# Seven-product form in the output projection and in two of three FFN-output stages

## The chip, the cores and the metric

One core of one Trainium2 chip runs the kernel, as one launch. The metric is the device time of one execution in microseconds (us). Repeated runs of the kernel before agree within 0.11% (1417.35 to 1418.89 us).

## What is computed

One encoder layer over 256 tokens and 2048 channels, all float32:

```
h   = rms_norm(x);  proj = h @ w_in            # q/k/v of three attention mixers and three gates
merged = sum over branches of sigmoid(gate_i) * (attention_i @ w_br_i)
x   = x + merged @ w_o                         # output projection, 2048 x 2048
hf  = rms_norm(x) @ w_ffn_in                   # 2048 -> 2 * 5632
x   = x + (silu(hf[:, :5632]) * hf[:, 5632:]) @ w_ffn_out   # 5632 -> 2048
```

## The kernel before

**Precision.** TensorE multiplies in a reduced float32 format. So each operand is held as a rounded part `hi` and a remainder `lo`, and one product of a 128x128 stationary tile by a 128x512 moving tile is three matmuls: hi·hi, hi·lo, lo·hi (`mul` in `pair`). The activations are stationary, transposed (channels on partitions); the weights move. Weight tiles arrive as 512 KB loads (`raw`, two k-tiles of 512 columns). `halves` splits each into `whi` (a copy on ScalarE, ACT, L351) and `wlo` (a subtraction on VectorE, DVE, L352).

**A pair.** `pair` makes the product of all 256 tokens (two token tiles t) with two column blocks c of 512, over k in pairs u of k-tiles. One u in one c is a *whole* step: 2 k-tiles x 2 token tiles x 3 = 12 matmuls; steps `du` and `Du` are c = 0 and 1. The four results lie in the PSUM banks Y, V (c = 0) and Z, Q (c = 1).

**The seven-product form.** For one u, the two k-tiles, two token tiles and two column blocks are a 2x2 by 2x2 block product: eight products, 24 matmuls, by the steps d and D. The form of Strassen and Winograd makes do with seven, 21 matmuls, at the price of sums. The step `f` makes two products (banks X, Y) from the c = 0 weights. `g` makes three DVE sums of weights (L441 to L443), then two products (W, Z). `h` makes one more sum (L457) and one product (V). `p` and `q` make the last two products (both X) from the sums kept in `t2` and `t3`, for up to two u at once. The stationary operands of W, Z and X are sums of token blocks, the *forms*; `stationary_forms` makes them in advance (L706 to L712, then a split). At the end of such a pair X is copied three times and W once (ACT, L392), DVE subtracts twice (L475, L478), and `sums` adds these to Y, V, Z, Q (L399, L400), so that `done` finds its result in SBUF. Without seven-product steps `done` reads PSUM itself.

**Order.** A pair's steps are a list (`STEPS`, `STEPS_GATE`, `STEPS_FFN`; `whole_k` has only d and D). `run` emits what a step needs (load, sums, split) three steps (`AHEAD`) before its matmuls; there are four buffers each of `whi` and `wlo`, and six of `raw`. Matmuls and SyncE's loads keep program order; `nc.follow` keeps the weight sums and splits of one engine in order; a planner places everything else. `tick` advances one side job after each step: work that follows a pair, such as the transposes, is such a job, under high priority.

**Stages around the change.** `merging`: gate pairs (3 of 8 u in seven-product form) and branch pairs. `projecting`: two pairs by `w_o`, all whole steps; its `add` adds the result to x (L764), then x is squared (ACT, L770), transposed and split into x1T (L124, L125). `feeding`: three groups of hidden columns (4, 4 and 3 pairs by `w_ffn`, all with 3 of 8 u in seven-product form); after each group two pairs by `w_ffn_out`, all whole steps, whose `output` adds the result to x (L818). The hidden activations are transposed by `transposed` and split into hT (L121, L122).

Of the kernel before, what the change touches and what calls it, by code (L numbers as in the profile page):

```python
# [49 lines left out]

SEVEN = (1, 2, 3)
STEPS = "d0 f1 D0 g1 d4 h1 f2 D4 g2 d5 h2 f3 D5 g3 d6 h3 p0 p2 D6 q0 q2 d7 D7".split()
STEPS_GATE = "d0 D0 d4 D4 f1 d5 g1 D5 h1 f2 g2 d6 h2 f3 g3 h3 p0 p2 D6 q0 q2 d7 D7".split()
STEPS_FFN = "d0 D0 f1 d4 g1 D4 h1 f2 d5 g2 D5 h2 f3 d6 g3 h3 p0 p2 D6 q0 q2 d7 D7".split()
AHEAD = 3


# [38 lines left out]
def encoder_block(ctx: ExitStack, tc: tile.TileContext, a: dict, out: bass.AP):  # L98
# [12 lines left out]
    def s4(shape, name, dt=F32):  # L111
        return mid.tile(shape, dt, name=name, tag="s4")
# [148 lines left out]
        row_scale(sr, r)  # L261
        known.add(name)

    def transposed(src, dst, g=None, lag=1):

        for h in range(2):
            if h:
                yield lag
            tp = bank("tp", "mm" if h and nc.on else "at")
            for k in range(2):  # L270
                for t in range(T):
                    nc.tensor.transpose(tp[:, k * S + t * P:k * S + (t + 1) * P],
                                        src[t][:, (2 * h + k) * P:(2 * h + k + 1) * P], ident)
# [82 lines left out]
    def pair(src, lhs, order, done, forms=None, operand=None):  # L356
# [5 lines left out]

        seven = sum(o[0] == "f" for o in order)
        left = {"X": 3 * seven}
        for o in order:
            for b in {"f": "Y", "g": "WZ", "h": "V", "d": "YV" * 2, "D": "ZQ" * 2}.get(o[0], ""):
# [69 lines left out]
        def second(u):  # L438
            def ready():
                b1, b2 = held[u]  # L440
                nc.follow(nc.vector.tensor_add(t3[:, SEVEN.index(u)], b2[:, 0], b2[:, 1]))  # L441
                nc.follow(nc.vector.tensor_add(b2[:, 0], b2[:, 0], b1[:, 0]))  # L442
                nc.follow(nc.vector.tensor_add(t2[:, SEVEN.index(u)], b2[:, 0], b2[:, 1]))  # L443
                hi, lo = halves(b2)

                def products():
                    mul("W", forms(u, 0), hi[:, 0], lo[:, 0])
                    mul("Z", forms(u, 2), hi[:, 1], lo[:, 1])
                    if left["W"] == 0:
                        copy(("B", 1), "W")  # L450
                return products
            return ready

        def third(u):
            def ready():
                b1 = held.pop(u)[0]
                nc.follow(nc.vector.tensor_add(b1[:, 1], t2[:, SEVEN.index(u)], b1[:, 1]))  # L457
                hi, lo = halves(b1[:, 1])
                return lambda: mul("V", at(2 * u + 1, 1), hi[:, 0], lo[:, 0])
            return ready  # L460

        def rest(o, v):
            tt, f = (t2, 1) if o == "p" else (t3, 3)
            n = min(2, seven - v)

            def ready():
                hi, lo = halves(tt[:, v:v + n])

                def products():
                    for i in range(n):  # L470
                        mul("X", forms(SEVEN[v + i], f), hi[:, i], lo[:, i])
                    if v + n == seven:
                        if o == "p":
# [217 lines left out]
    mT, x1T, x = [], [], []  # L691
    ss1 = const.tile([P, T, 4], F32, name="ss1")

    def stationary_forms(lhs, pool=None):


        n = len(SEVEN)
        fh = s8([P, 4, n, P], "fh", pool=pool)
        fl = s8([P, 4, n, P], "fl", pool=pool)
        raw = s8([P, 4, n, P], "fraw", F32)  # L700
        full = s8([P, 2 * n, S], "ffull", F32)

        def steps():
            for i, u in enumerate(SEVEN):
                for k in range(2):
                    nc.vector.tensor_add(full[:, 2 * i + k], *(v.bitcast(F32) for v in lhs(2 * u + k)))  # L706
            yield 1
            b = full.rearrange("p (u k) (t s) -> p k t u s", k=2, t=2)
            nc.vector.tensor_sub(raw[:, 0], b[:, 0, 1], b[:, 1, 1])
            nc.vector.tensor_sub(raw[:, 3], b[:, 0, 0], b[:, 0, 1])  # L710
            nc.vector.tensor_sub(raw[:, 1], raw[:, 0], b[:, 0, 0])
            nc.vector.tensor_add(raw[:, 2], raw[:, 1], b[:, 1, 0])  # L712
            yield 1
            split(fh, fl, raw)
        start(steps())
        return lambda u, f: (fh[:, f, SEVEN.index(u)], fl[:, f, SEVEN.index(u)])

    def merging():
        forms = stationary_forms(xT, tail)
        for b, (g0, k0, k1) in enumerate(((8, 2, 6), (4, 6, 12))):  # L720
            for j in (0, 2):
                sg = [None, None]
# [29 lines left out]
    forms = []  # L752


    def projecting():
        x.extend(s8([P, D], f"x{t}", F32) for t in range(T))
        for t in range(T):
            nc.sync.dma_start(out=x[t], in_=a["x"][t * P:(t + 1) * P, :])
        x1T.extend(s8([P, 2, 4, S], "x1T") for _ in range(4))
        for n in (0, 2):  # L760
            def add(c, r, n=n):
                xc = [x[t][:, (n + c) * NC:(n + c + 1) * NC] for t in range(T)]
                for t in range(T):
                    nc.vector.tensor_add(xc[t], r[t], xc[t])  # L764

                def later():
                    yield 1
                    sq = s4([P, T, NC], "sq")
                    for t in range(T):
                        nc.scalar.activation(sq[:, t], xc[t], AF.Square, accum_out=ss1[:, t, n + c:n + c + 1])  # L770
                    yield 2
                    yield from transposed(xc, lambda k, m: (x1T[n + c][:, 0, k], x1T[n + c][:, 1, k]),
                                          lambda k: gT[:, 2, 4 * (n + c) + k:4 * (n + c) + k + 1], 2)
                    if n + c == 1:
                        forms.append(stationary_forms(x1l))
                    elif n + c == 3:
                        yield 2
                        ssr = small.tile([P, T], F32, name="ss", bufs=1)
                        nc.vector.tensor_reduce(ssr, ss1, axis=AX.X, op=ALU.add)
                        row_scale(ssr, r_f)  # L780
                start(urgent(later()))
            yield pair(block_pair(a["w_o"], n), lambda k: (mT[k // 4][:, 0, k % 4], mT[k // 4][:, 1, k % 4]),
                       whole_k(KT // 2), add)


    def feeding():
        for c0, c1 in ((0, 4), (4, 8), (8, KF // 4)):
            hT = []
            for n in range(c0, c1):
                halves_of = []  # L790

                def hidden(c, v, av=halves_of):
                    if c == 0:
                        av.append(v)
                        for t in range(T):
# [6 lines left out]
                    def later():  # L802
# [1 line left out]
                        nc.vector.tensor_mul(av, av, bv)  # L804
                        yield 3
                        yield from transposed([av[:, t] for t in range(T)],
                                              lambda k, m: (tl[:, 0, k:k + m], tl[:, 1, k:k + m]), lag=2)
                    start(urgent(later()))
                yield pair(lambda u, c, n=n: a["w_ffn"][n][2 * u + c], x1l, STEPS if n else STEPS_FFN, hidden,
                           lambda u, f: forms[0](u, f))  # L810
            last = c1 == KF // 4
            for n in (0, 2):
                def output(c, r, n=n, last=last):
                    for t in range(T):
                        for h in range(2 if last and n + c == 3 else 1):
                            w = NC if not (last and n + c == 3) else NC // 2
                            o = slice((n + c) * NC + h * w, (n + c) * NC + (h + 1) * w)
                            nc.vector.scalar_tensor_tensor(x[t][:, o], r[t][:, h * w:(h + 1) * w],  # L818
                                                           r_f[:, 0, t:t + 1], x[t][:, o],
                                                           op0=ALU.mult, op1=ALU.add)  # L820
                            if last:
                                nc.sync.dma_start(out=out[t * P:(t + 1) * P, o], in_=x[t][:, o])
                yield pair(lambda u, c, n=n, c0=c0: a["w_ffn_out"][n + c][2 * c0 + u],
                           lambda k, hT=hT: (hT[k // 4][:, 0, k % 4], hT[k // 4][:, 1, k % 4]),
                           whole_k(2 * (c1 - c0)), output)

    def everything():
        for stage in (merging, projecting, feeding):
# [88 lines left out]
```

## Time and profile before

| | |
|---|---|
| runs | 1417.35, 1418.86, 1418.89 us; median 1418.86 |
| the profiled execution | 1419.69 us, of which the span of the profile is 1417.9 us |
| PE busy | 1395.6 us, 98% of the span |
| DVE busy | 1033.6 us, 73% |
| ACT busy | 764.9 us, 54% |
| memory traffic | 277 MB, 195 GB/s |

Matmuls overlap in the profile: one of 128x512 is shown as some 0.39 us, but the next begins 0.23 us after it. A matmul's cost is therefore read as the distance between starts. A busy share is an average over the stretch that it stands for.

### The profile page before, as it was taken

What the parts mean: (1) busy time and instruction counts of PE and PEld (TensorE: products, weight loads), DVE (VectorE), ACT (ScalarE), POOL (GpSimd) and SP (SyncE); (2) the same over time, 40 slices, a digit from 0 to 9 for tenths busy, and PEclk for the clock granted to TensorE, in tenths of its full rate; (3) what the DMA queues carried; (4) which work ended last, traced back from release to release, by engine and by line L of the source; (5) the groups of instructions that cost most, each with busy time, mean ns of one, the idle gap of its engine ahead of it and who ended that gap; (6) DMA issues with size and microseconds to landing.
All of it is one profiled execution on the core that took longest, in us unless ns stands there. A gap on an engine that the chain in (4) does not pass through costs nothing.

```text
span 1417.9 us, 17330 instructions
## 1 busy us (share of the span) xinstructions
PE 1395.6 (98%) x6287; PEld 1144.8 (81%) x6287; DVE 1033.6 (73%) x1305; ACT 764.9 (54%) x1026; POOL 76.7 (5%) x146
## 2 busy tenths in 40 slices
PE   8999999999999999999999999999999999999998
PEld 6778878888878888888878888888888888888886
DVE  5767756765588887767788897548889845788854
ACT  6766546644464564645565556335566633465632
POOL 0024533200000000000000000000000000000000
PEclk9999999999999999999999999999999999999999
DMA  8976535546565675765555666665566666555644
GB/s 287 334 240 212 161 109 190 157 154 195 178 196 178 193 225 173 273 187 180 175 183 192 203 193 213 192 193 181 191 193 204 215 190 193 180 191 191 221 127 174
DMA packets 79414, 277.07 MB, mean 195 GB/s; under 512 B 8992, under 2 KB 11552, under 8 KB 79072
## 3 DMA queue, kind: packets, MB, share of 16 engines
q1 hardware_dynamic: 79184, 275.94, 60.1%
q8 instruction: 49, 0.80, 0.2%
q14 instruction: 37, 0.30, 0.1%
q10 hardware_dynamic: 144, 0.02, 0.0%
HBM read 273.05 MB, written 2.88 MB: 195 GB/s over the span
## 4 chain that ended last, share of the span: by engine, by line
PE 84%; DVE 5%; ACT 3%; issue 3%; DMA 2%; POOL 2%; SPq 0%; ACTq 0%; DVEq 0%; POOLq 0%
PE mm L73 17%; PE mmZ L73 15%; PE mmV L73 14%; PE mmY L73 14%; PE mmQ L73 13%; PE mmX L73 6%; DVE wlo L352 3%; ACT whi L351 2%; PE mmW L73 2%; DMA raw<-in_w_mem 1%; PE tp L73 1%; PE sc L73 1%; POOL rot L571 1%; DVE raw L442 1%; DVE t L441 1%
## 5 line engine op out<-in xcount | busy, mean ns | idle before, releaser
L352 DVE TENSOR_TENSOR wlo<-raw,whi 128x1024 fp32r<-128x1024 f32 (+1 forms) x441 | 509.6, 1168 | 249.1 <-ACT whi L351 245.0
L351 ACT ACTIVATE whi<-raw 128x1024 fp32r<-128x1024 f32 (+1 forms) x441 | 437.4, 1013 | 403.0 <-PE mmV L73 133.7
L73 PE MATMUL mm<-whi,xT 128*128 128x512 f32 x768 | 243.9, 394 | 0.0
L122 DVE TENSOR_TENSOR wlo<-raw,whi 128x1024 fp32r<-128x1024 f32 x100 | 128.5, 1295 | 80.8 <-ACT whi L121 80.6
L73 PEld LDWEIGHTS mm<-whi,xT 128*128 128x128 f32 x768 | 144.0, 189 | 29.5 <-issue 0.8
L121 ACT ACTIVATE whi<-raw 128x1024 fp32r<-128x1024 f32 x100 | 105.7, 1070 | 88.1 <-PE mm L73 81.4
L73 PE MATMUL mm<-wlo,xT 128*128 128x512 f32 x384 | 150.7, 393 | 0.0
L73 PE MATMUL mmY<-whi,x1T 128*128 128x512 f32 x286 | 111.2, 390 | 0.0
L73 PE MATMUL mmV<-whi,x1T 128*128 128x512 f32 x286 | 108.6, 392 | 0.0
L73 PE MATMUL mmZ<-whi,x1T 128*128 128x512 f32 x220 | 85.7, 389 | 0.0
L73 PE MATMUL mmQ<-whi,x1T 128*128 128x512 f32 x220 | 85.6, 389 | 0.0
L73 PEld LDWEIGHTS mm<-wlo,xT 128*128 128x128 f32 x384 | 72.5, 189 | 15.7 <-issue 0.8
L73 PE MATMUL mmZ<-whi,hT 128*128 128x512 f32 x176 | 69.6, 395 | 0.0
L73 PE MATMUL mmQ<-whi,hT 128*128 128x512 f32 x176 | 69.1, 393 | 0.0
L73 PE MATMUL mmV<-whi,hT 128*128 128x512 f32 x176 | 69.1, 392 | 0.0
L73 PE MATMUL mmY<-whi,hT 128*128 128x512 f32 x176 | 69.1, 392 | 0.0
L73 PEld LDWEIGHTS mmY<-whi,x1T 128*128 128x128 f32 x286 | 53.7, 188 | 11.3
L73 PEld LDWEIGHTS mmV<-whi,x1T 128*128 128x128 f32 x286 | 53.7, 188 | 11.1 <-ACT whi L351 0.2
L352 DVE TENSOR_TENSOR wlo<-t,whi 128x1024 fp32r<-128x1024 f32 (+1 forms) x60 | 54.7, 953 | 3.9 <-ACT whi L351 3.9
L73 PE MATMUL mmV<-wlo,x1T 128*128 128x512 f32 x143 | 55.8, 390 | 0.2 <-DVE wlo L352 0.2
L73 PE MATMUL mmY<-wlo,x1T 128*128 128x512 f32 x143 | 55.7, 389 | 0.0
L351 ACT ACTIVATE whi<-t 128x1024 fp32r<-128x1024 f32 (+1 forms) x60 | 48.5, 834 | 0.0
(254 smaller groups left out, 2620.1 us busy)
## 6 DMA issues: line engine op xcount, KB each, us to landing
raw<-in_w_ffn SPq DMA_DIRECT2D x176, 512.0 KB, 3.7
raw<-in_w_gate SPq DMA_DIRECT2D x96, 512.0 KB, 4.1
raw<-in_w_ffn_out SPq DMA_DIRECT2D x88, 512.0 KB, 3.8
raw<-in_w_qkv SPq DMA_DIRECT2D x64, 512.0 KB, 4.6
raw<-in_w_o SPq DMA_DIRECT2D x32, 512.0 KB, 3.6
raw<-in_w_br SPq DMA_DIRECT2D x24, 512.0 KB, 3.7
raw<-in_w_mem SPq DMA_DIRECT2D x16, 512.0 KB, 6.6
rawT<-in_memT SPq DMA_DIRECT2D x8, 256.0 KB, 4.8
```

Source lines behind the costliest of these rows:

```text
L73: ins = op(*args, **kw)
L121: nc.scalar.activation(hi, src, AF.Copy)
L122: nc.vector.tensor_sub(lo, src, hi.bitcast(F32))
L351: nc.follow(nc.scalar.activation(hi[:, o], v, AF.Copy))
L352: nc.follow(nc.vector.tensor_sub(lo[:, o], v, hi[:, o].bitcast(F32)))
L441: nc.follow(nc.vector.tensor_add(t3[:, SEVEN.index(u)], b2[:, 0], b2[:, 1]))
L442: nc.follow(nc.vector.tensor_add(b2[:, 0], b2[:, 0], b1[:, 0]))
L571: op(ov[:, :, :, c], ov[:, :, :, c], tmp[:, :n])
```

## The change

Two seven-product steps (u = 2 and 3) take the place of four whole steps in both pairs of the output projection; two (u = 6, 7) and three (u = 5, 6, 7) in the two output pairs of the first and second FFN group. The third group's output pairs stay. The forms are now made one u at a time by `token_sums`, in four small operations and a split, in tiles of their own. For u = 6 and 7 of the hidden activations they are made from the transposes in PSUM (`also`); for the others from hi + lo.

```diff
-SEVEN = (1, 2, 3)
+STEPS_O = "d0 D0 d1 D1 f2 d4 g2 D4 h2 d5 f3 D5 g3 d6 h3 p0 D6 q0 d7 D7".split()
+STEPS_OUT = "d0 D0 d1 D1 d2 D2 f6 d3 g6 D3 h6 f7 d4 g7 h7 p0 D4 q0 d5 D5".split()
+STEPS_OUT2 = "d0 f5 D0 g5 d1 h5 f6 D1 g6 d2 h6 f7 D2 g7 d3 h7 p0 p2 D3 q0 q2 d4 D4".split()
...
-    def transposed(src, dst, g=None, lag=1):
+    def transposed(src, dst, g=None, lag=1, also=None):
...
                 split(d[0], d[1], tp.rearrange("p (k s) -> p k s", s=S))
+                if also:
+                    full = s4([P, 4, P], "ffull")
+                    nc.scalar.activation(full, tp.rearrange("p (b s) -> p b s", s=P), AF.Copy)
+                    also(h, full)
...
-    def stationary_forms(lhs, pool=None):
...
+    def token_sums(full, to):
+        raw = s4([P, 4, P], "fraw")
+        nc.vector.tensor_sub(raw[:, :2], full[:, :2], full[:, 1::2])
+        nc.vector.tensor_sub(raw[:, 2], raw[:, 1], full[:, 0])
+        nc.vector.tensor_add(raw[:, 3], raw[:, 2], full[:, 2])
+        split(to[:, 0], to[:, 1], raw)
+
+    def sums_of(lhs, these, room):
         def steps():
+            for u, to in zip(these, room):
+                full = s4([P, 4, P], "ffull")
                 for k in range(2):
+                    nc.vector.tensor_add(full[:, 2 * k:2 * k + 2].rearrange("p t s -> p (t s)"),
+                                         *(v.bitcast(F32) for v in lhs(2 * u + k)))
+                token_sums(full, to)
+                yield 1
         start(steps())
+        return by_pair(these, room)
...
     def merging():
-        forms = stationary_forms(xT, tail)
+        forms = sums_of(xT, (1, 2, 3), form_room(3, tail))
...
     def projecting():
+        oforms = sums_of(mTl, (2, 3), form_room(2))
...
-                    nc.vector.tensor_add(xc[t], r[t], xc[t])
+                    nc.vector.tensor_add(xc[t], r[:, t], xc[t])
...
-                        forms.append(stationary_forms(x1l))
+                        room.extend(form_room(3))
+                        forms.append(sums_of(x1l, (1, 2, 3), room[:3]))
...
-            yield pair(block_pair(a["w_o"], n), lambda k: (mT[k // 4][:, 0, k % 4], mT[k // 4][:, 1, k % 4]),
-                       whole_k(KT // 2), add)
+            yield pair(block_pair(a["w_o"], n), mTl, STEPS_O, add, oforms)
...
     def feeding():
+            late = [] if last else form_room(2)
...
                         yield from transposed([av[:, t] for t in range(T)],
-                                              lambda k, m: (tl[:, 0, k:k + m], tl[:, 1, k:k + m]), lag=2)
+                                              lambda k, m: (tl[:, 0, k:k + m], tl[:, 1, k:k + m]), lag=2,
+                                              also=late and (lambda h, v: token_sums(v, late[h])))
...
+            pairs = whole_k(2 * (c1 - c0)), whole_k(2 * (c1 - c0))
+            out_forms = None
+            if not last:
+                pairs = STEPS_OUT, STEPS_OUT2
+                sums_of(hTl, (5,), room[3:])
+                out_forms = by_pair((5, 6, 7), room[3:] + late)
...
-                           whole_k(2 * (c1 - c0)), output)
+                yield pair(lambda u, c, n=n, c0=c0: a["w_ffn_out"][n + c][2 * c0 + u], hTl, pairs[n // 2], output,
+                           out_forms)
```

## Rows read from the trace of the kernel before

**Rows 1.** The page's first part: engine, busy us, share of the span, instructions
```profile
span 1417.9 us, 17330 instructions
PE 1395.6 (98%) x6287; PEld 1144.8 (81%) x6287; DVE 1033.6 (73%) x1305; ACT 764.9 (54%) x1026; POOL 76.7 (5%) x146
```

**Rows 2.** Windows: stretch, length, busy PE, PEld, DVE, ACT, POOL (instructions), PE clock, DMA share, GB/s
```profile
605.60:651.00 45.40, 45.40 (x208) 37.29 (x208) 25.89 (x27) 19.98 (x24) 0.00 (x0) 1.00 0.60 187
651.00:697.20 46.20, 46.20 (x212) 37.99 (x211) 31.88 (x41) 24.02 (x35) 0.00 (x0) 1.00 0.58 185
871.00:915.40 44.40, 44.40 (x200) 36.46 (x199) 24.61 (x24) 18.02 (x19) 0.00 (x0) 1.00 0.64 197
915.40:959.80 44.40, 44.40 (x196) 36.43 (x195) 22.70 (x22) 16.96 (x16) 0.00 (x0) 1.00 0.56 181
1044.80:1087.30 42.50, 42.38 (x191) 34.75 (x190) 37.57 (x44) 25.59 (x31) 0.00 (x0) 1.00 0.62 198
```

**Rows 3.** PE in order of time, projection: start, shown length, instruction
```profile
640.42 0.39 PE L73 MATMUL mmY<-whi,mT 128*128 128x512 f32 x1
...
645.92 0.39 PE L73 MATMUL mmY<-whi,mT 128*128 128x512 f32 x1
```

**Rows 4.** PE in order of time: g3 of a later hidden pair, then the first hidden pair
```profile
767.79 0.39 PE L73 MATMUL mmW<-whi,fh 128*128 128x512 f32 x1
...
768.64 0.39 PE L73 MATMUL mmW<-whi,fl 128*128 128x512 f32 x1
...
728.07 0.42 PE L73 MATMUL mmV<-whi,x1T 128*128 128x512 f32 x1
728.71 0.50 PE L73 MATMUL mmV<-wlo,x1T 128*128 128x512 f32 x1 [0.23 <-DVE wlo L352]
...
729.29 0.40 PE L73 MATMUL mmX<-whi,fh 128*128 128x512 f32 x1
730.19 0.50 PE L73 MATMUL mmX<-wlo,fh 128*128 128x512 f32 x1 [0.50 <-DVE wlo L352]
```

**Rows 5.** Groups by line: matmuls of the form tiles in 15 pairs with 45 such steps
```profile
L73 PE MATMUL mmX<-wlo,fh 128*128 128x512 f32 x90 | 35.4, 394 | 0.5 <-DVE wlo L352 0.5
L73 PE MATMUL mmW<-wlo,fh 128*128 128x512 f32 x45 | 19.0, 423 | 2.4 <-DVE wlo L352 1.4
```

**Rows 6.** DVE groups by shape: count | busy us, mean ns | idle before, releaser
```profile
L352 DVE TENSOR_TENSOR wlo<-raw,whi 128x1024 fp32r<-128x1024 f32 x396 | 478.6, 1222 | 222.1 <-ACT whi L351 218.0
L441 DVE TENSOR_TENSOR t<-raw 128x512 f32<-128x512 f32 x45 | 30.8, 684 | 0.0
L706 DVE TENSOR_TENSOR ffull<-x1T 128x256 f32<-128x256 f32 x6 | 2.4, 421 | 0.1
L608 DVE TENSOR_SCALAR nm<-mx 128x2 f32<-128x2 f32 x12 | 1.9, 158 | 0.0
```

**Rows 7.** DVE in order of time, instructions without idle time between them
```profile
1129.13 1.22 DVE L352 TENSOR_TENSOR wlo<-raw,whi 128x1024 fp32r<-128x1024 f32 x1
1130.27 0.68 DVE L399 TENSOR_TENSOR SB<-mmZ,SB 128x512 f32<-128x512 f32 x1
1130.87 0.68 DVE L400 TENSOR_TENSOR SB<-mmQ,SB 128x512 f32<-128x512 f32 x1
```

**Rows 8.** DVE in order of time before the merging stage, with idle time in brackets
```profile
327.51 1.23 DVE L122 TENSOR_TENSOR wlo<-raw,whi 128x1024 fp32r<-128x1024 f32 x1 [2.02 <-ACT whi L121]
```

**Rows 9.** ACT groups by shape, as in rows 6
```profile
L351 ACT ACTIVATE whi<-raw 128x1024 fp32r<-128x1024 f32 x396 | 411.7, 1056 | 350.1 <-PE mmV L73 133.7 <-PE mmQ L73 110.1 <-DVE raw L442 59.5
L392 ACT ACTIVATE SA<-mmX 128x512 f32<-128x512 f32 x30 | 17.7, 589 | 25.4 <-PE mmX L73 25.4
```

**Rows 10.** First gate pair: PE in order of time, then the stretch around it
```profile
405.91 0.49 PE L73 MATMUL mmW<-whi,fh 128*128 128x512 f32 x1 [0.95 <-ACT whi L351]
407.17 0.50 PE L73 MATMUL mmW<-wlo,fh 128*128 128x512 f32 x1 [0.77 <-DVE wlo L352]
...
408.00:412.00 4.00, 4.00 (x13) 2.88 (x12) 3.15 (x4) 4.00 (x6) 0.00 (x0) 0.62 0.80 238
```

More of the change, by code (lines that the diff above doesn't have):

```diff
@@ L356, in pair @@
     def pair(src, lhs, order, done, forms=None, operand=None):
-        seven = sum(o[0] == "f" for o in order)
+        those = [int(o[1:]) for o in order if o[0] == "f"]
+        seven = len(those)
         left = {"X": 3 * seven}
@@ L440, in ready @@
                 b1, b2 = held[u]
-                nc.follow(nc.vector.tensor_add(t3[:, SEVEN.index(u)], b2[:, 0], b2[:, 1]))
+                nc.follow(nc.vector.tensor_add(t3[:, those.index(u)], b2[:, 0], b2[:, 1]))
                 nc.follow(nc.vector.tensor_add(b2[:, 0], b2[:, 0], b1[:, 0]))
-                nc.follow(nc.vector.tensor_add(t2[:, SEVEN.index(u)], b2[:, 0], b2[:, 1]))
+                nc.follow(nc.vector.tensor_add(t2[:, those.index(u)], b2[:, 0], b2[:, 1]))
                 hi, lo = halves(b2)
@@ L456, in ready @@
                 b1 = held.pop(u)[0]
-                nc.follow(nc.vector.tensor_add(b1[:, 1], t2[:, SEVEN.index(u)], b1[:, 1]))
+                nc.follow(nc.vector.tensor_add(b1[:, 1], t2[:, those.index(u)], b1[:, 1]))
                 hi, lo = halves(b1[:, 1])
@@ L470, in products @@
                     for i in range(n):
-                        mul("X", forms(SEVEN[v + i], f), hi[:, i], lo[:, i])
+                        mul("X", forms(those[v + i], f), hi[:, i], lo[:, i])
                     if v + n == seven:
@@ L692, in encoder_block, with by_pair, form_room @@
     ss1 = const.tile([P, T, 4], F32, name="ss1")
-    def stationary_forms(lhs, pool=None):
[L697 to L701, printed above, removed]
+    def token_sums(full, to):
[5 more added lines that the diff above has]
+    def sums_of(lhs, these, room):
         def steps():
-            for i, u in enumerate(SEVEN):
+            for u, to in zip(these, room):
+                full = s4([P, 4, P], "ffull")
                 for k in range(2):
[L706 to L714, printed above, removed]
-        start(steps())
-        return lambda u, f: (fh[:, f, SEVEN.index(u)], fl[:, f, SEVEN.index(u)])
+                    nc.vector.tensor_add(full[:, 2 * k:2 * k + 2].rearrange("p t s -> p (t s)"),
+                                         *(v.bitcast(F32) for v in lhs(2 * u + k)))
+                token_sums(full, to)
+                yield 1
+        start(steps())
+        return by_pair(these, room)
+    def by_pair(these, room):
+        return lambda u, f: (room[these.index(u)][:, 0, (f + 1) % 4], room[these.index(u)][:, 1, (f + 1) % 4])
+    def form_room(n, pool=None):
+        tiles = [s8([P, 2, 2, 4, P], "forms", pool=pool) for _ in range((n + 1) // 2)]
+        return [tiles[i // 2][:, i % 2] for i in range(2 * len(tiles))]
     def merging():
-        forms = stationary_forms(xT, tail)
+        forms = sums_of(xT, (1, 2, 3), form_room(3, tail))
         for b, (g0, k0, k1) in enumerate(((8, 2, 6), (4, 6, 12))):
@@ L751, in encoder_block @@
     x1l = lambda k: (x1T[k // 4][:, 0, k % 4], x1T[k // 4][:, 1, k % 4])
-    forms = []
+    forms, room = [], []
     def projecting():
@@ L759, in projecting @@
         x1T.extend(s8([P, 2, 4, S], "x1T") for _ in range(4))
+        mTl = lambda k: (mT[k // 4][:, 0, k % 4], mT[k // 4][:, 1, k % 4])
+        oforms = sums_of(mTl, (2, 3), form_room(2))
         for n in (0, 2):
@@ L788, in feeding, with hidden @@
             hT = []
+            last = c1 == KF // 4
+            hTl = lambda k, hT=hT: (hT[k // 4][:, 0, k % 4], hT[k // 4][:, 1, k % 4])
+            late = [] if last else form_room(2)
             for n in range(c0, c1):
                 halves_of = []
-                def hidden(c, v, av=halves_of):
+                def hidden(c, v, av=halves_of, late=late if n == c1 - 1 else []):
                     if c == 0:
@@ L810, in feeding @@
                            lambda u, f: forms[0](u, f))
-            last = c1 == KF // 4
+            pairs = whole_k(2 * (c1 - c0)), whole_k(2 * (c1 - c0))
[4 more added lines that the diff above has]
+                out_forms = by_pair((5, 6, 7), room[3:] + late)
             for n in (0, 2):
@@ L814, in output @@
                     for t in range(T):
+                        rt = r[t] if last else r[:, t]
                         for h in range(2 if last and n + c == 3 else 1):
@@ L817, in output @@
                             o = slice((n + c) * NC + h * w, (n + c) * NC + (h + 1) * w)
-                            nc.vector.scalar_tensor_tensor(x[t][:, o], r[t][:, h * w:(h + 1) * w],
+                            nc.vector.scalar_tensor_tensor(x[t][:, o], rt[:, h * w:(h + 1) * w],
                                                            r_f[:, 0, t:t + 1], x[t][:, o],
@@ L822, in output @@
                                 nc.sync.dma_start(out=out[t * P:(t + 1) * P, o], in_=x[t][:, o])
-                yield pair(lambda u, c, n=n, c0=c0: a["w_ffn_out"][n + c][2 * c0 + u],
-                           lambda k, hT=hT: (hT[k // 4][:, 0, k % 4], hT[k // 4][:, 1, k % 4]),
-                           whole_k(2 * (c1 - c0)), output)
+                yield pair(lambda u, c, n=n, c0=c0: a["w_ffn_out"][n + c][2 * c0 + u], hTl, pairs[n // 2], output,
+                           out_forms)
     def everything():
```

## The prediction

> **What bounds the kernel now.** I read the page's engine totals first: PE is busy 98% of the span [rows 1]. A busy PE need not be a PE at its pace, so the next view is PE in order of time, in the stages that the change touches. In the projection 24 matmuls of 128x512 start within 5.50 us, 0.229 us apart, with no wait [rows 3]. The windows then say who is near to being late: PE is busy throughout, DVE for 25.89 of 45.40 and 31.88 of 46.20 us in the projection, and for 24.61 and 22.70 of 44.40 us in an output stage's two pairs [rows 2]. So these stages last as long as their matmuls do, and DVE has 40% room. A hidden pair, with three of eight u in seven-product form, is the model of what they become: DVE busy for 37.57 of 42.50 us [rows 2], and one small wait of PE for a `wlo` split in g3: two starts on, 768.64 − 767.79 − 2 x 0.229 = 0.39 us late [rows 4].
>
> **What is taken away.** The group rows show that a seven-product step is really 21 matmuls: for 45 of them there are 90 form matmuls in X and 45 in W of each kind [rows 5]; together with Y, V, Z and the two-sided X that is seven products of three. Two whole steps are 24. The change makes 2 + 2 such steps in the projection and 2 x (2 + 3) in the outputs, 14 in all, so it removes 14 x 3 = 42 matmuls. At 0.229 us that is **−9.62 us**, all on the path while PE stays the bound.
>
> **What is added on DVE.** Back to back, a 1024-column instruction takes 1130.27 − 1129.13 = 1.14 us and a 512-column one 0.60 us [rows 7], less than their shown 1.22 and 0.68 us [rows 6], because the next starts before the last has ended. A seven-product step needs f 1.14, g 3 x 0.60 + 1.14, h 2 x 0.60: 5.28 us. p and q need 1.14 each when they serve two u, 0.60 each for a third. The two whole steps that go had 2.28 us.
> - Pair with two: 2 x 5.28 + 2.28 − 4.56 = 8.28. At its end come two subtractions and four additions, 6 x 0.60 = 3.60. Sum +11.9 us.
> - Pair with three: 3 x 5.28 + 3.48 − 6.84 = 12.48, and 3.60. Sum +16.1 us.
> - Token sums, no row before: one 256-long operation at 0.42, two 128-long ones each between 0.16 (2 elements) and 0.42 [rows 6], one 512-long split at 0.60: 1.3 to 1.9 us, I take 1.6, the middle, as 128 lies between the two rows; from hi + lo two more of 0.42, so 2.4 us.
>
> Projection: 25.89 + 31.88 + 2 x 11.9 + 2 x 2.4 = 86.4 us of DVE in 91.6 − 12 x 0.229 = 88.9 us. The old share holds 68 instructions [rows 2] that mostly had idle time before them; queued tight each is 0.08 us shorter, 5.4 us in all, which leaves 81 us, 91%. An output stage: 24.61 + 22.70 + 11.9 + 16.1 + 2.4 + 2 x 1.6 = 80.9, less 46 x 0.08 = 3.7, so 77.2 us in 88.8 − 15 x 0.229 = 85.4 us, 90%. The hidden pair runs at 88% and loses 0.4 us. So I expect PE to stay the bound, with small waits.
>
> The Trainium skill has a rule against this (VectorE: DVE Perf Modes, "The DRAIN you can't avoid"): the next operation does not start until the pipeline of the last has emptied. Taken as the whole shown length, it would make DVE's new work dearer, with the result under the first rival. The trace disagrees where instructions are queued tight: 0.68 us shown, 0.60 us from start to start [rows 7].
>
> **What is added elsewhere.** ACT, per pair with two: splits 2 x (2 x 1.06 + 0.63) + 2 x 1.05 − 4 x 1.06 = 3.4 (0.63 taken as little over the 0.59 of a 512-column copy), and four copies of 0.59: +5.8 us [rows 9]. On the 44.0 us of the projection [rows 2] that makes 56 of 89 us with the forms' splits, 63%: beside PE, 0. Loads: the same 512 KB tiles in the same number on SyncE's queue, each pair's two tiles of a seven-product step held from f to h, as a hidden pair does at 0.62 of the DMA engines [rows 2]: 0. Transposes: no more of them; the extra ACT copy keeps their bank about 0.6 us longer, with six steps until g6 asks for the sums: 0. The forms of the gate pairs: the sums are cut finer (per step three times 2.4 us against six adds, four sums and a split before), at a place where DVE idles 2.02 us before a split [rows 8]: 0, at most ±0.5 us. The additions into x come two DVE operations (1.2 us) later at a pair's end, and the transposes that read x stand three steps, 36 x 0.229 = 8.2 us, behind it: 0 while DVE's queue is no fuller than that; without that cover the 1.2 us shows once per pair.
>
> **New waits.** Behind a late `wlo` stand, on PE, all later matmuls, so each wait counts in full. The trace has two sizes: 0.4 us a pair for the order f D g d h p p (`STEPS`), and for the denser end h f d g h p of the first hidden pair 728.71 − 728.07 − 0.23 = 0.41 and 730.19 − 729.29 − 0.23 = 0.67 us, with an estimated 0.1 us for the start behind each 1.3 us [rows 4].
> - `STEPS_OUT2` is `STEPS` with other numbers: 0.4 us in each of two pairs (0 to 1.3).
> - `STEPS_OUT` has that dense end, but p for one pair of u only, and no splits of x1T beside it: between 0.4 and 1.3, I take 0.85, twice: 1.7 us (0.8 to 2.6).
> - First projection pair 0.4 (0 to 1.3). The second has the x1T splits and three token sums (7.2 us) in its first half: 0.8 (0.4 to 2).
> - First hidden pair: its 1.3 us grow as DVE enters it with more queued: +0.4 (0 to 1.3).
>
> Sum 4.1 us, ends 1.2 to 9.8. **Net −9.6 + 4.1 = −5.5 us** on the profiled execution's 1419.69 us, 1414.2; that execution is 0.83 us above the median, so 1413.4 us for the median. No wait at all would give 1409.2.
>
> **Rivals.**
> 1. *DVE becomes the bound* (or the planner, short of 8 KB or 4 KB tiles for forms, t2, t3 and the late sums, delays its sums, with the same sign). For: 90% is an average, and g brings 2.94 us of DVE to 1.37 us of PE at once. With whole durations instead of starts a pair with two costs 13.4 and one with three 18.1 us; the projection comes to 57.8 + 26.8 + 5 = 89.6 of 88.9 us, an output stage to 47.3 + 31.5 + 6 = 84.8 of 85.4. Against: rows 7, and 88% at 0.4 us. Then all six new pairs lose the dense 1.3 us at least, −9.6 + 7.8 = −1.8 us, and the three that are fullest (second projection pair, `STEPS_OUT` twice) up to 2 us, −9.6 + 3 x 1.3 + 3 x 2 = +0.3 us: 1417.1 to 1419.2, I take 1417.7.
> 2. *Slower: the waits bring TensorE's clock down.* In the first gate pair two waits 1.2 us apart, 0.95 us and 1.26 − 0.23 = 1.03 us, are followed by a mean granted clock of 0.62 from 408 to 412, so part of it at 1.2 GHz [rows 10]. That place cost 2.0 + 0.38 x 4 = 3.5 us. If the same happened in four places (second projection pair, first hidden pair, both `STEPS_OUT`), with 0.4 us in the other three pairs: 14.0 + 1.2 − 9.6 = +5.6 us, 1424.5. From the third place on, (9.6 − 1.2) / 3.5 = 2.4, the kernel is slower. Against: 0.41 and 0.67 us in the first hidden pair left the next matmuls at 0.40 us shown [rows 4], the full clock; none of my waits reaches 1 us twice running. The Trainium skill names the mechanism (TensorE: Matmul & The Clock Gate, "HAM oscillation"): waits between bursts send the clock down, and each burst pays again. Rows 10 agree.
> 3. *It doesn't save what it says*: if PE's pace were set by loads or by `whi` buffers, 42 fewer matmuls would save nothing. Rows 3 speak against it: no start is late over 24 matmuls. I give it no chance of its own.
>
> **Chances.** Forecast 0.70, rival 1 0.21, rival 2 0.09. A measurement of this kernel tells 0.2%, 2.8 us, from no change. The forecast's own range is 1409 to 1416, all of it faster by that. Of rival 1, 0.04 is faster, 0.15 within, 0.02 slower; rival 2 is slower. So faster 0.74, same 0.15, slower 0.11. The range goes from no wait, 1409, to past rival 1, 1420.
>
> **What would show it.** Right: PE has 42 fewer matmuls; each projection pair is 0.6 to 1 us shorter, each output stage 2 us; DVE is at about 90% in both, and PE's waits for `wlo` in them sum to 2 to 6 us. Wrong: a wait of PE over 1 us in the second projection pair or at h7 or p0 of `STEPS_OUT`, a granted clock under 1.00 after 605 us, or a PE pitch over 0.229 us in these stages.

## The result, and the profile after

The changed kernel takes **1421.43 us** (median of 11 executions, 1418.98 to 1424.29); the kernel before, on the same chip, 1418.36 (11 executions, 1416.63 to 1418.89). The ratio is **1.0024 [1.0015, 1.0034]**: slower by 0.24%, where I forecast 0.4% faster, and above my range. The profiled execution took 1424.29 us, the longest of the eleven, so the stage lengths below add up to 1.5 us more than the medians differ by.

The page of the changed kernel, its first part and the head of its chain; to be set beside [rows 1]:

```profile
span 1422.5 us, 17528 instructions
PE 1392.6 (98%) x6245; PEld 1136.5 (80%) x6245; DVE 1125.9 (79%) x1481; ACT 804.5 (57%) x1096; POOL 76.7 (5%) x146
...
PE 75%; DVE 10%; ACT 5%; issue 5%; DMA 2%; POOL 2%; SPq 0%; ACTq 0%; DVEq 0%; POOLq 0%
```

The change does what it says: 6287 − 6245 = 42 matmuls fewer, and PE is busy 3.0 us less. DVE has 92.3 us more work, and the share of DVE in the chain of waits is 10% (5% before). The span is longer all the same, so PE stands idle or slow somewhere. The windows say where: one stage each, with the columns of [rows 2]. After (projection, its second pair, hidden group 1, output 1, hidden 2, output 2, hidden 3):

```profile
606.10:694.90 88.80, 88.80 (x406) 72.93 (x405) 77.99 (x106) 53.81 (x73) 0.00 (x0) 1.00 0.60 188
650.50:694.90 44.40, 44.40 (x204) 36.39 (x203) 42.27 (x65) 29.11 (x44) 0.00 (x0) 1.00 0.59 188
694.90:872.70 177.80, 174.08 (x774) 141.93 (x773) 157.91 (x206) 108.19 (x139) 0.00 (x0) 0.99 0.59 188
872.70:960.10 87.40, 86.38 (x379) 69.75 (x378) 75.03 (x91) 48.12 (x58) 0.00 (x0) 1.00 0.62 193
960.10:1132.10 172.00, 170.71 (x757) 139.20 (x756) 153.83 (x184) 101.59 (x123) 0.00 (x0) 1.00 0.62 196
1132.10:1219.60 87.50, 86.48 (x379) 69.79 (x379) 75.07 (x91) 48.19 (x58) 0.00 (x0) 1.00 0.62 191
1219.60:1348.80 129.20, 127.99 (x567) 104.27 (x566) 114.16 (x134) 75.75 (x91) 0.00 (x0) 1.00 0.62 196
```

The same stages before (hidden 1, output 1 as a whole, hidden 2):

```profile
697.20:871.00 173.80, 172.56 (x774) 140.97 (x773) 153.41 (x196) 107.07 (x135) 0.00 (x0) 1.00 0.60 191
871.00:959.80 88.80, 88.80 (x394) 72.89 (x393) 47.31 (x45) 34.98 (x35) 0.00 (x0) 1.00 0.60 189
959.80:1129.90 170.10, 169.73 (x758) 139.54 (x757) 149.13 (x173) 101.20 (x122) 0.00 (x0) 1.00 0.62 198
```

All stages, each read from such a window of its kernel (the last two columns are experiments told below):

| us | before | after | early sum (run 4) | early sum, both later g (run 10) |
|---|---|---|---|---|
| ahead of the projection | 605.6 | 606.1 | 600.5 | 599.3 |
| projection | 91.6 | 88.8 | 89.1 | 89.1 |
| hidden 1 | 173.8 | 177.8 | 176.0 | 172.9 |
| output 1 | 88.8 | 87.4 | 85.7 | 85.7 |
| hidden 2 | 170.1 | 172.0 | 169.9 | 168.8 |
| output 2 | 88.8 | 87.5 | 85.7 | 85.9 |
| hidden 3 | 127.2 | 129.2 | 127.5 | 126.4 |
| rest, to the span's end | 72.0 | 73.7 | 73.4 | 73.0 |
| span | 1417.9 | 1422.5 | 1407.8 | 1401.1 |

Read the column of after against before. The projection gives 2.8 us, all of its 12 x 0.229. Each output stage gives 1.35 us of its 15 x 0.229 = 3.44. And **the hidden stages, whose matmuls and order of steps were not touched, take 4.0, 1.9 and 2.0 us more.** The new token sums (`also`) fall into hidden 1 and 2, but hidden 3 has none of them and loses as much as hidden 2. The first and the last row (+0.5 and +1.7) are outside the changed stages and move by as much between kernels whose code there is the same: 603.4 us (run 2) to 606.1 ahead of the projection, 71.9 (run 6) to 73.7 at the end.

PE's waits, grouped by tile and releaser (us in total, times, longest), of after; in the trace of before the three groups were 1.4 us in 3, none, and 0.5 us in 1:

```profile
PE mmW L75 <- DVE wlo L359: 4.2, 11, 0.8
...
PE mmW L75 <- DVE x1T L127: 2.6, 1, 2.6
PE mmX L75 <- DVE wlo L359: 2.5, 5, 0.5
```

They are two different things. In the changed kernel's lines the copy and the split are L358 and L359, the sums of g L449 to L451, that of h L465. PE in order of time shows both kinds of wait, first at g1 of the first hidden pair, then at g in two turns of output 1's second pair:

```profile
703.09 0.60 PE L75 MATMUL tp<-ident,x 128*128 128x128 f32 x4
703.45 0.48 PE L75 MATMUL mmY<-whi,x1T 128*128 128x512 f32 x1
...
706.31 0.60 PE L75 MATMUL tp<-ident,x 128*128 128x128 f32 x4
709.48 0.77 PE L75 MATMUL mmW<-whi,forms 128*128 128x512 f32 x1 [2.58 <-DVE x1T L127]
...
710.47 0.63 PE L75 MATMUL mmW<-whi,forms 128*128 128x512 f32 x1
710.90 0.63 PE L75 MATMUL mmZ<-whi,forms 128*128 128x512 f32 x1
...
933.48 0.50 PE L75 MATMUL mmW<-wlo,forms 128*128 128x512 f32 x1 [0.16 <-DVE wlo L359]
...
943.04 0.50 PE L75 MATMUL mmW<-wlo,forms 128*128 128x512 f32 x1 [0.34 <-DVE wlo L359]
```

**The first hidden pair.** Four transposes take 703.45 − 703.09 = 0.36 us, so W should have started at 706.67; it starts 2.81 us late, once. Its releaser is a split of `x1T` on DVE, yet W doesn't read that tile: it reads `forms` and `whi`. The second half of a transposed tile takes its PSUM bank from the same set (`"mm"`) as W, V and Q (the two `bank` calls in `transposed` and in `mul`), and that bank is free only when its split is done. After the wait the matmuls start 0.43 us apart instead of 0.23, which is the lower of TensorE's two levels, 1.2 GHz; the granted clock of 709 to 713 is 0.58. DVE at that time, then DVE and ACT in output 1:

```profile
707.65 1.23 DVE L359 TENSOR_TENSOR wlo<-raw,whi 128x1024 fp32r<-128x1024 f32 x1 [0.22 <-ACT whi L358]
708.79 0.15 DVE L139 SCALAR_TENSOR_TENSOR rs_t<-rs_y 128x2 f32<-128x2 f32 x1
708.86 0.48 DVE L127 SCALAR_TENSOR_TENSOR x1T<-tp,gT,x1T 128x256 fp32r<-128x256 f32 x1
...
929.52 0.68 DVE L449 TENSOR_TENSOR t<-raw 128x512 f32<-128x512 f32 x1
930.24 0.69 DVE L450 TENSOR_TENSOR raw<-raw 128x512 f32<-128x512 f32 x1
930.97 0.69 DVE L451 TENSOR_TENSOR t<-raw 128x512 f32<-128x512 f32 x1
932.20 2.36 DVE L359 TENSOR_TENSOR wlo<-raw,whi 128x1024 fp32r<-128x1024 f32 x2 [0.54 <-ACT whi L358]
934.48 0.69 DVE L465 TENSOR_TENSOR raw<-t,raw 128x512 f32<-128x512 f32 x1
935.94 0.69 DVE L359 TENSOR_TENSOR wlo<-raw,whi 128x512 fp32r<-128x512 f32 x1 [0.78 <-ACT whi L358]
936.89 2.36 DVE L359 TENSOR_TENSOR wlo<-raw,whi 128x1024 fp32r<-128x1024 f32 x2 [0.26 <-ACT whi L358]
939.17 0.68 DVE L449 TENSOR_TENSOR t<-raw 128x512 f32<-128x512 f32 x1
...
935.28 2.53 ACT L358 ACTIVATE whi<-raw 128x512 fp32r<-128x512 f32 x3 [2.16 <-DVE raw L465]
```

The split that begins at 708.86 ends at 709.34, and W starts 0.14 us behind that end; in runs 1, 4, 5 and 7 below it starts 0.15 us behind the end of such a split as well. Ahead of the split in DVE's queue stand weight splits and the row scale's small operations.

**The output pairs.** The lower half of that fence is one turn of `f D g d h` in the second pair of output 1: 939.17 − 929.52 = **9.65 us of DVE**. In the same turn PE issues 39 matmuls (W and Z, d, V, X and Y, D), 39 x 0.229 = 8.93 us. DVE is not at work all that time: for 0.54 + 0.78 + 0.26 = 1.58 us it waits for ACT. The sum for h (L465) and the `wlo` split of it (L359) stand next to each other in DVE's queue, with the `whi` copy on ACT between them. So ACT first stands idle for 2.16 us until the sum is there, with the copies for the next steps queued behind, and then DVE waits 0.78 us for the copy. Each such turn takes 0.7 us off the lead that DVE has over PE, until a matmul has to wait for its `wlo`. Such waits stand at X in p0 of the first output pair (906.27, [0.51 <-DVE wlo L359]), at W in the second (933.48, 943.04), and at W in the hidden pair behind (967.34, 976.99, 986.55), where the late starts come to about 1.7 us.

### The profile page after: what moved, and what is told of

Same layout as the page of the kernel before. It is cut to its first block, busy times and chain, and to the rows that moved or that the text cites. A ratio compares the mean times of both kernels' runs of the same rounds, so it can differ in the third digit from the quotient of the medians.

```text
span 1422.5 us, 17528 instructions
## 1 busy us (share of the span) xinstructions
PE 1392.6 (98%) x6245; PEld 1136.5 (80%) x6245; DVE 1125.9 (79%) x1481; ACT 804.5 (57%) x1096; POOL 76.7 (5%) x146
## 4 chain that ended last, share of the span: by engine, by line
PE 75%; DVE 10%; ACT 5%; issue 5%; DMA 2%; POOL 2%; SPq 0%; ACTq 0%; DVEq 0%; POOLq 0%
PE mm L75 17%; PE mmZ L75 12%; PE mmY L75 11%; PE mmV L75 11%; PE mmQ L75 10%; PE mmX L75 7%; DVE wlo L359 5%; ACT whi L358 4%; PE mmW L75 2%; DMA raw<-in_w_mem 1%; DVE raw L450 1%; PE tp L75 1%; DVE t L449 1%; PE sc L75 1%; POOL rot L579 1%
## 5 line engine op out<-in xcount | busy, mean ns | idle before, releaser
L359 DVE TENSOR_TENSOR wlo<-raw,whi 128x1024 fp32r<-128x1024 f32 (+1 forms) x455 | 518.0, 1153 | 154.1 <-ACT whi L358 149.2
L358 ACT ACTIVATE whi<-raw 128x1024 fp32r<-128x1024 f32 (+1 forms) x455 | 444.7, 1001 | 340.8 <-DVE raw L450 74.5
L75 PE MATMUL mmQ<-whi,x1T 128*128 128x512 f32 x220 | 85.7, 389 | 0.0
L75 PE MATMUL mmX<-whi,forms 128*128 128x512 f32 x236 | 79.7, 390 | 0.0
L359 DVE TENSOR_TENSOR wlo<-t,whi 128x1024 fp32r<-128x1024 f32 x76 | 72.2, 982 | 4.8 <-ACT whi L358 4.6
L358 ACT ACTIVATE whi<-t 128x1024 fp32r<-128x1024 f32 x76 | 63.4, 858 | 1.2 <-PE mmX L75 0.7
L75 PE MATMUL mmY<-whi,hT 128*128 128x512 f32 x156 | 60.4, 391 | 0.0
L75 PE MATMUL mmV<-whi,hT 128*128 128x512 f32 x156 | 60.1, 392 | 0.0
L75 PE MATMUL mmZ<-whi,hT 128*128 128x512 f32 x136 | 53.9, 396 | 1.3 <-ACT whi L358 1.3
```

The source lines that it names most:

```text
L75: ins = op(*args, **kw)
L358: nc.follow(nc.scalar.activation(hi[:, o], v, AF.Copy))
L359: nc.follow(nc.vector.tensor_sub(lo[:, o], v, hi[:, o].bitcast(F32)))
```

## The experiments

They are called run 1 to run 11 below. The expectations stand as they were written before each run, and give the theories letters. Those that decide: A, waits in and behind the changed pairs eat the gain, in the projection and in the outputs apart; C, the finer token sums cost it; D, the order of the sum for h against ACT's copy makes the outputs late; F, the first hidden pair's wait only moves when its order changes; H, a later g ends the wait behind the outputs. In runs 6, 7 and 11 the letter A stands for the theory named there. Medians are of 11 executions where nothing else is said, ratios against the kernel before on the same chip.

**1. The projection alone.** Output pairs whole again:

```
-            late = [] if last else form_room(2)
+            late = []
...
-            if not last:
+            if False:
...
-                        rt = r[t] if last else r[:, t]
+                        rt = r[t]
```

> The two projection pairs keep their seven-product steps (12 matmuls fewer); the output pairs are whole steps again. Theory A (each part loses at a place of its own): the projection gains 2.75 us as in the profile after, and the first hidden pair loses 4.0 us, because W's PSUM bank is held by the x1T transposes whose splits are late on VectorE, and the clock drops after that wait of 2.8 us: +1.3 us against before, between -0.5 and +2.5. Rival B (the 2.8 us wait is an accident of one profiled run): -2.4 us, no clock drop near 708 us.

1419.35 us, 1.0004 [0.9996, 1.0013]. The projection takes 88.8 us, hidden 1 176.4 instead of 173.8, everything behind as before. W waits 2.58 us for `x1T` at 708.30 here too, though the granted clock of 708 to 712 stays 1.00. What twelve matmuls give, the next stage takes. So the wait is no accident of one profiled run.

**2. The outputs alone.** The projection whole again:

```
-        oforms = sums_of(mTl, (2, 3), form_room(2))
...
-                    nc.vector.tensor_add(xc[t], r[:, t], xc[t])
+                    nc.vector.tensor_add(xc[t], r[t], xc[t])
...
-            yield pair(block_pair(a["w_o"], n), mTl, STEPS_O, add, oforms)
+            yield pair(block_pair(a["w_o"], n), mTl, whole_k(KT // 2), add)
```

> The four output pairs keep their ten seven-product steps (30 matmuls fewer); the projection is whole steps again. Theory A: each output stage gains 1.4 us and the hidden pair behind it loses 2.0 us, as in the profile after: +1.1 us against before, up to +2.9 if the last output stage is late again by 1.8. Rival B (the loss sits in the projection and the first hidden pair): -2.8 us or better, with no waits for wlo in the hidden pair behind an output stage.

1419.43 us, 1.0005 [0.9996, 1.0013]. Hidden 1 is as before (173.9), the outputs take 87.4 us each, the hidden stages behind them 172.1 and 129.1: −2.75 + 3.9. Thirty matmuls fewer gain nothing.

**3. Neither, only the finer token sums** of the gate and hidden pairs (both edits above):

> No new seven-product steps: only the token sums of the gate and hidden pairs are made in the new way, one u at a time in 4 KB tiles. Theory A: within 0.7 us of before. Rival C (the finer token sums and their tiles cost something themselves): +1 us or more, with a wait of PE in the first hidden or first gate pair that the kernel before does not have.

1418.07 us, 0.9997 [0.9987, 1.0006]. The token sums cost nothing, as I had it.

**4. The early sum.** In the changed kernel the sum for h moves from h's own step into g's, behind the other three. The same additions, of the same size:

```
 second(u):   nc.follow(nc.vector.tensor_add(t2[:, those.index(u)], b2[:, 0], b2[:, 1]))
+             nc.follow(nc.vector.tensor_add(b1[:, 1], t2[:, those.index(u)], b1[:, 1]))
 third(u):
-             nc.follow(nc.vector.tensor_add(b1[:, 1], t2[:, those.index(u)], b1[:, 1]))
```

> The whole change, with one VectorE addition moved: the sum that h needs (b1 + t2) is made in g, right after t2, in place of at the head of h. The work is the same. Theory D (VectorE is not short of time but waits for ScalarE: sum, then the whi copy, then the wlo split, 0.78 us idle in every seven-product step, so a u takes VectorE 9.6 us against 8.9 us of matmuls): the waits at g go, 2.0 us in each output stage, 1.7 us in each hidden pair behind one, 0.4 us in each other hidden pair: 1421.4 - 8 to - 11, so 1410 to 1413. Rival E (VectorE's work itself is the bound): 1421.4, within 1 us.

**1408.46 us** (5 executions), **0.9924 [0.9912, 0.9937]**. The same turn on DVE, in order of time:

```profile
920.33 0.68 DVE L449 TENSOR_TENSOR t<-raw 128x512 f32<-128x512 f32 x1
921.05 0.69 DVE L450 TENSOR_TENSOR raw<-raw 128x512 f32<-128x512 f32 x1
921.78 0.69 DVE L451 TENSOR_TENSOR t<-raw 128x512 f32<-128x512 f32 x1
922.50 0.69 DVE L452 TENSOR_TENSOR raw<-t,raw 128x512 f32<-128x512 f32 x1
923.11 2.96 DVE L359 TENSOR_TENSOR wlo<-raw,whi 128x1024 fp32r<-128x1024 f32 x3
926.62 2.56 DVE L359 TENSOR_TENSOR wlo<-raw,whi 128x1024 fp32r<-128x1024 f32 x2 [0.55 <-ACT whi L358]
929.10 0.68 DVE L449 TENSOR_TENSOR t<-raw 128x512 f32<-128x512 f32 x1
```

and its windows of output 1 and hidden 2:

```profile
865.60:951.30 85.70, 85.54 (x378) 70.00 (x377) 74.73 (x91) 48.32 (x58) 0.00 (x0) 1.00 0.59 196
951.30:1121.20 169.90, 169.10 (x757) 139.67 (x756) 153.31 (x184) 101.85 (x123) 0.00 (x0) 1.00 0.61 198
```

The turn takes 929.10 − 920.33 = 8.77 us instead of 9.65, now under PE's 8.93. DVE's busy time in the output stage is the same, 74.73 against 75.03 us, and the stage is 1.7 us shorter, hidden 2 2.1 us. This run shows the mechanism: not the amount of DVE's work, but its order against ACT. The time ahead of the projection falls by 5.6 us as well; 5.2 of it lie behind the start of the first gate pair (377.2 us in the changed kernel, 376.8 here), and gate pairs have such turns in the kernel before too. The 2.97 us wait of the first hidden pair is still there.

**5. The same edit on the kernel before.**

> The kernel before with h's addition made in g, nothing else of the change. Theory D (VectorE's idle time behind ScalarE in each seven-product step is what makes PE wait): the gate pairs and hidden pairs lose their waits too, 3 + 0.6 + 0.6 us in the gate pairs and 0.4 us in each of ten hidden pairs with 1 us in the first: 1418.4 - 9, between 1408 and 1411. Rival G (the addition's place matters only with the new steps, where VectorE is full, and early_h's 10 us are the 42 matmuls at last): 1417 to 1418.5.

1411.66 us (5 executions), 0.9950 [0.9937, 0.9962]; I had expected 1409.4. Part of the miss has a name. In the first hidden pair, where the trace of before has no such wait, PE in order of time now shows this:

```profile
704.01 0.47 PE L73 MATMUL mmW<-whi,fh 128*128 128x512 f32 x1 [2.64 <-DVE x1T L125]
```

with a granted clock of 0.66 from 703.8 to 708, and hidden 1 takes 175.3 us, 1.5 more than before. The projection has no seven-product step in this kernel. So the wait doesn't need the new steps: the first hidden pair's own order allows it, and an edit elsewhere can bring it out.

**6. A later g1 in the first hidden pair** of the changed kernel:

```
-STEPS_FFN = "d0 D0 f1 d4 g1 D4 h1 f2 d5 g2 D5 h2 ...
+STEPS_FFN = "d0 D0 f1 d4 D4 g1 h1 f2 d5 D5 g2 h2 ...
```

> The whole change; in the first pair of each hidden group the whole steps D4 and D5 stand ahead of g1 and g2, one step earlier than now. Theory A (in the first hidden pair W waits 2.8 us for a PSUM bank that a transpose of x1T holds until its split on VectorE): 2.75 us of other matmuls fill that wait and the clock stays up: 1421.4 - 4, between 1416.5 and 1418.5. Rival F (W waits for its own sums or weights, so the wait moves along with it or to the next bank): 1421 or more, a wait of PE over 1.5 us in that pair.

1419.88 us, 1.0012 [1.0003, 1.0021]. The expectation took this list for the first pair of every hidden group; it serves the very first alone. There W's wait is gone, and the first X of f1 waits for a bank instead:

```profile
701.70 0.47 PE L75 MATMUL mmX<-whi,x1T 128*128 128x512 f32 x1 [1.57 <-DVE x1T L127]
```

The granted clock behind it (701.5 to 705.5) stays 1.00; hidden 1 takes 176.5 us, 1.3 less. The wait for the splits moved to an earlier user of a bank and shrank. The run saves 1.55 us of the 4 that theory A gave it; where part of the rest went, run 8 shows.

**7. The row scale started later** (`yield 12` for `yield 2` ahead of it), to take its twelve small operations out from between the splits.

> The whole change; the row scale of the hidden layer (a chain of twelve tiny VectorE operations of 0.16 us each, now between the splits of x1T) starts ten steps later. Theory A, with the splits late because of what stands ahead of them on VectorE: the bank wait of 2.8 us falls by 1 to 2 us and the clock stays up: 1418 to 1420. If the splits are late by their own chain with ScalarE and PE: 1421.4, the wait as before.

1421.71 us, 1.0019 [1.0011, 1.0028]. It tells nothing: the twelve operations came out at the same place in DVE's queue, and W waited 2.58 us as before.

**8. Early sum and later g1 together**, in the changed kernel:

> Both edits together on the whole change. If they act on different waits the gains add: early_h's 1408.5 and the 3.2 us bank wait with its clock drop of 1.7 us: 1403.5 to 1405. If VectorE's queue is behind both, less: 1407 to 1408.5.

1403.41 us (4 executions), 0.9892 [0.9879, 0.9906], at the low end of the forecast. But the gains more than add: the list alone saved 1.55 us (run 6), on top of the early sum it saves 5.05. Hidden 1 takes 172.9 us. In run 6 the later g brought new waits for `wlo` at the end of the same pair:

```profile
725.82 0.50 PE L75 MATMUL mmW<-wlo,forms 128*128 128x512 f32 x1 [0.45 <-DVE wlo L359]
...
727.88 0.50 PE L75 MATMUL mmV<-wlo,x1T 128*128 128x512 f32 x1 [0.22 <-DVE wlo L359]
```

Here, with the early sum, 0.03 us of such a wait is left (720.22). So the two edits are not independent.

**9. Both on the kernel before**, so that the change can be weighed in an order that suits it:

> The kernel before with both edits: h's addition in g, and D4 ahead of g1 in the very first hidden pair (no other hidden pair uses that list). It is what early_g1_late's 1403.4 us has to be held against: the difference is the change itself. From before_early's profile the bank wait of 2.9 us and the clock drop of 1.7 us shrink to 1.8 us: 1411.7 - 2.8 = 1408.9. If the change is then worth its matmuls less small waits (projection 2.5, output stages 3 each, less 1.1 in each hidden pair behind them): 1403.4 + 6.3 = 1409.7. Rival (the change gains nothing even now): 1403 to 1405.

1409.69 us (5 executions), 0.9947 [0.9934, 0.9961]. Against the last run the change itself is worth 0.9892 / 0.9947, **0.55% or 7.8 us** by the ratios, whose intervals, taken as independent, leave 5 to 10 us. The two medians differ by 6.3 us, and the two profiles by 5.2 us from the first gate pair on. So the 42 matmuls, which last 9.6 us, give some 5 to 8 us in this order.

**10. A later g behind the outputs.** Run 8 still waits about 1 us for `wlo` at a g of the hidden pair behind each output stage. That pair gets its own list: `d0 D0 f1 d4`, 42 matmuls, stand ahead of g1, where `STEPS` has `d0 f1 D0`, 30:

```
+STEPS_NEXT = "d0 D0 f1 d4 g1 D4 h1 f2 d5 g2 D5 h2 f3 d6 g3 h3 p0 p2 D6 q0 q2 d7 D7".split()
-  ... STEPS if n else STEPS_FFN, ...
+  ... STEPS_FFN if not n else STEPS_NEXT if n == c0 else STEPS, ...
```

> early_g1_late, and in the hidden pair behind each output stage the first seven-product step starts two steps later (d0 D0 f1 d4 g1 in place of d0 f1 D0 g1). Theory H (there W waits 0.96 us for wlo, since the sums of the output pair and its additions into x stand ahead of g1 on VectorE): both waits go, -2.1 us: 1401.3. Rival (the wait moves to the next g): 1403.4.

**1402.36 us** (4 executions), **0.9890 [0.9876, 0.9903]**, the shortest of all: 16 us under before, 19 under the changed kernel. Windows of hidden 1 and hidden 2, then PE's waits:

```profile
688.40:861.30 172.90, 171.30 (x774) 141.28 (x773) 157.54 (x206) 109.08 (x139) 0.00 (x0) 1.00 0.59 194
...
947.00:1115.80 168.80, 168.80 (x757) 139.77 (x756) 153.61 (x184) 102.27 (x123) 0.00 (x0) 1.00 0.60 200
```

```profile
PE mmX L76 <- DVE x1T L128: 1.6, 1, 1.6
...
PE mmW L76 <- DVE wlo L360: 0.7, 3, 0.4
```

In hidden 2 PE is busy from end to end; of 4.2 + 2.5 us of waits for `wlo` in W and X 0.7 are left. Against run 8 hidden 2 and hidden 3 are 1.1 us shorter each (169.9 and 127.5 there): 168.8 and 126.4 us, what they take in run 5, whose output pairs are whole. So nothing of the loss behind the outputs is left. The medians, 1.05 us apart, have intervals that overlap, so the stages show this gain and the total can't.

**11. d4 and D4 ahead of f1 in the first hidden pair**, on top of run 10, to take its last 1.6 us away. The later whole steps move up too, and D6 no longer stands between p and q:

```
-STEPS_FFN = "d0 D0 f1 d4 D4 g1 h1 f2 d5 D5 g2 h2 f3 d6 g3 h3 p0 p2 D6 q0 q2 d7 D7".split()
+STEPS_FFN = "d0 D0 d4 D4 f1 d5 g1 D5 h1 f2 d6 g2 h2 f3 D6 g3 h3 p0 p2 q0 q2 d7 D7".split()
```

> next_g1, and in the very first hidden pair d4 D4 stand ahead of f1 as well. Theory A (X waits 1.78 us for a bank held by a transpose of x1T): that wait goes, -1.8 us more: 1399.5. Rival (d4 then waits for x1T itself, whose splits are no earlier): 1401 to 1402.

1404.47 us (4 executions), 0.9906 [0.9892, 0.9919]: not faster. PE in order of time has two waits there now:

```profile
699.20 0.50 PE L76 MATMUL mmY<-whi,x1T 128*128 128x512 f32 x1 [1.26 <-DVE x1T L128]
...
728.48 0.50 PE L76 MATMUL mmX<-whi,forms 128*128 128x512 f32 x1 [0.96 <-ACT SB L401]
```

Y of d4 reads the third `x1T` tile, whose split is not done yet: here a direct reader waits for the late splits, as the rival had it. The second wait is of the edit's own making: X at q0 now stands right behind p2 and waits for the copy of X (L401), which D6 used to cover.

## Why the prediction was wrong

- **What goes: right.** 42 matmuls at 0.229 us; the projection shows 12 of them in full, the output stages under the early sum 3.1 of 3.44 us each.
- **DVE's work: sized right, and on the high side.** I had 81 and 77.2 us for the projection and an output stage; they are 78.0 and 75.0. The finer token sums cost nothing (run 3). No wait of PE in the changed kernel is put down to a load. ACT I had as "beside PE, 0"; its share was no cost, but its place in the order was, as the next point tells.
- **"DVE has 40% room", "The hidden pair runs at 88% and loses 0.4 us": this step failed.** I took idle time of DVE for room. At 75.0 of 87.4 us, 86%, it was already too slow, because 1.58 us of each turn are waits for ACT in the middle of its queue. Run 4 shows it: the same work in another order, and most of the waits go. The trace of before could have told me: nearly all of DVE's idle time ahead of `wlo` splits, 218.0 of 222.1 us, is released by ACT [rows 6]. The view that I lacked is a turn's length on DVE against the same turn on PE, here in the second hidden pair of the kernel before:

```profile
754.16 0.68 DVE L441 TENSOR_TENSOR t<-raw 128x512 f32<-128x512 f32 x1
...
757.46 2.36 DVE L352 TENSOR_TENSOR wlo<-raw,whi 128x1024 fp32r<-128x1024 f32 x2 [0.45 <-ACT whi L351]
...
761.20 0.69 DVE L352 TENSOR_TENSOR wlo<-raw,whi 128x512 fp32r<-128x512 f32 x1 [0.78 <-ACT whi L351]
762.15 2.36 DVE L352 TENSOR_TENSOR wlo<-raw,whi 128x1024 fp32r<-128x1024 f32 x2 [0.26 <-ACT whi L351]
764.43 0.69 DVE L441 TENSOR_TENSOR t<-raw 128x512 f32<-128x512 f32 x1
```

  That is 10.27 us of DVE, a split of `hT` among them and 1.49 us idle behind ACT, against 8.93 us for 39 matmuls and 0.36 us for four transposes on PE. So in such a turn DVE already fell behind PE. That it gets by at 88% because it enters with a lead, and that the output pairs enter without one, is my reading; no run shows it by itself.
- **Waits in the changed pairs: wrong in each, near in the sum.** I put 1.25 us on an output stage; it had 2.1 (3.44 − 1.35). I put 1.2 us on the projection; it had none, with DVE busy for 42.27 of 44.40 us in its second pair. So a high share by itself did not bring a wait either. In all I had 3.7 us here against 4.1 measured (9.6 − 2.8 − 1.4 − 1.3); that these are close is luck.
- **What comes behind was missing: the term that made the sum wrong.** I costed the changed pairs, and behind them only +0.4 us in the first hidden pair. The lead that an output stage no longer leaves cost 1.9 and 2.0 us in the hidden stages behind (back to 169.9 and 127.5 us in run 4). The first hidden pair cost 4.0: a wait of 2.8 us and matmuls at half pace. For it I had the "+0.4 (0 to 1.3)" and a 0 for x that comes later to the transposes that read it. The 0.6 us for which a copy holds a bank longer I weighed for the hidden activations' transposes alone; I didn't ask who waits for the banks of the x1T transposes. Together 7.9 us stand behind the changed pairs, where the sum had 0.4.
- **The sum by stages**, profile against profile: +0.5 ahead, −2.8 projection, +4.0, −1.4, +1.9, −1.3, +2.0, +1.7 for the rest, 4.6 us. My term for new waits was 4.1 us with an upper end of 9.8; all that stood against the 9.6 came to 14.2: 4.1 in the changed pairs, 7.9 behind them, and 2.2 in the first and the last stretch, where kernels of the same code differ by as much.
- **The rivals.** Rival 1 had the right sign of error and the wrong rule: no engine was full. Rival 2's mechanism came in one place, behind a bank, not behind a `wlo`; it did not bring the clock down in four. Of my signs of being wrong one came, a granted clock under 1.00 after 605 us; no wait in the changed pairs reached 1 us, so I had looked for the rest in the wrong stages.

Open: what sets the splits of `x1T` back in the first hidden pair (run 7 could not move what stands between them); that W waits for the bank rests on the code, on its start right behind the end of a split in five kernels and on run 6, where another user of a bank waits in its place; no run took the bank alone away; and why the stretch behind the last hidden stage moves by 1.7 us.

## What to carry to other kernels

An engine's share of busy time says little where two engines hand each tile to and fro in order: take one turn of the loop in the trace, from an instruction to the same instruction of the next turn, on each engine, and compare the lengths. When work that was in the pipeline's slack is used up, look for the bill in the stages behind, whose code is unchanged. And before work is dropped or added, look for a producer that stands right ahead of its consumer's wait: moving one addition up by a step was worth 0.5% in the kernel before and, by 0.9924 against 1.0024, 1.0% in the changed one, where the 42 matmuls saved are worth about 0.55% in an order that suits them.

## What was unexpected of the hardware

- DVE's dependent sums don't overlap. Independent 512-column additions start 0.60 us apart at 0.68 shown [rows 7]; the three of g, each of which reads or overwrites a tile that the one ahead wrote or read, start 0.72 apart (929.52, 930.24, 930.97), and the split behind the fourth, of another tile, 0.61 (922.50 to 923.11). The rule that I set aside (the Trainium skill, VectorE: DVE Perf Modes, "The DRAIN you can't avoid") thus agrees with the trace for these and not for the others. The same section adds that a next operation which is not held starts earlier, as the others do.
- Much the same wait did not always bring TensorE's clock down: 2.58 us at 709.48 gave 0.58 behind it and in run 7 0.57, 2.58 us at 708.30 in run 1 gave 1.00, 2.64 us in run 5 gave 0.66, 1.57 us in run 6 gave 1.00.
